# Hybrid decoder step: the recurrence's pairs 32 and 64 tokens apart in one round instead of two

## The chip, the cores and the metric

The kernel runs on one core of a Trainium2 chip. The metric is device time in microseconds (us) of one execution of the whole program. Of each kernel one execution was also recorded by the hardware profiler; its views are quoted below. PE is TensorE, DVE is VectorE, ACT is ScalarE, POOL is GpSimd, SP is SyncE, and PEld is TensorE's loading of weights.

## The reference

A two-layer decoder trunk over one prompt of 512 tokens and 8 samples of 4 tokens, 544 columns in all. Layer 0 mixes tokens by causal pooling, layer 1 by a gated linear recurrence (HGRN2) with 8 heads of 128 x 128 state; a gated ConvFFN follows each. The change lies in the recurrence of layer 1. Per head it computes, with `f` the gates, `k = 1 - f` up to bounds, and `b` the running sum of `log f`:

```python
b = jnp.cumsum(gc, axis=2)
o_inter = jnp.einsum('bhtd,bhde->bhte', qc * jnp.exp(b), S)
diff = b[:, :, :, None, :] - b[:, :, None, :, :]
decay = jnp.where(causal, jnp.exp(jnp.where(causal, diff, 0.0)), 0.0)
a = jnp.einsum('bhtd,bhsd,bhtsd->bhts', qc, kc, decay)
o = o_inter + jnp.einsum('bhts,bhse->bhte', a, vc)
```

So the score of a pair of tokens (t, s) is the product of q[t] and k[s] over 128 features, each multiplied by the product of all gates between s and t. The state S goes on from chunk to chunk with the chunk's whole gate product.

## The kernel before

Activations are kept transposed: features on the 128 partitions, tokens along the free axis. A projection block is a product of three TensorE matmuls per slice (helper `mm3`): weights and activations are split into a high and a low part in the float32r format, and high x high, high x low and low x high are added up. `block` runs that for 8 slices of 128 input features and two column halves of 256 and 288 columns, 48 matmuls into a tile `ps`. In the profile these are the rows with `ps<-xh,wh`, `ps<-xl,wh` and `ps<-xh,wl`.

The attention of a head works on four chunks of 128 tokens, tile `F` (gates), `K`, `q`, `v`. Decays are never divided out. Pairs are handled by their distance, in rounds that double: in the round of width w the chunk is cut into blocks of 2w tokens, and the K of the first half is multiplied with the q of the second half. `scale` then multiplies every second half of q with the gate product of the first half, and every first half of K with the product of the second, and `products` multiplies neighbouring gate products, so that `st["F"]` holds one product per block. `round_a` does distances up to 2 in one go (80 columns of a shared tile `q2`, called `z` there), `round_b` 4 and 8 (48 columns), and `level(w)` one width each: 16, 32, 64. A round's matmuls are plain float32 (two instructions each in the profile), and their 16, 32 or 64 output partitions make them use a column tile of TensorE: 32 or 64 of its 128 columns, at the position of their output partitions. In the profile's forms `128*32` is a matmul with 128 rows and a column tile of 32. ACT copies the scores to the tile `A` (128 x 4 x 128).

Behind the rounds, `ktrans` transposes K, `states` multiplies K with V (four full-width matmuls, `pa<-t` 128x128) and chains the chunks' states S on DVE, `output` adds A x V, q x S of the chunk before, and the samples' parts, which use `qm` and `As` on column tiles; then `sstates` and `back`.

The order of instructions isn't written out by hand. Every instruction is recorded in a list with its dependences and an estimated cost (`record`, `cost`), and `emit` goes through all engines with a simulated clock: of the instructions whose inputs and buffers are due first on an engine it takes the one with the longest remaining chain, and TensorE's recorded order counts as a part of that chain. The heads' stages are put into the list by `tick`, one of them for four `mm3` of the projection that runs meanwhile (`PACE` 0.25). So each engine's order is fixed when the program is built, and every engine works through its own list. All recorded instructions have the line of the one call in `emit`, L304.

Of the kernel before, what the change touches and what calls it, by code (L numbers as in the profile page):

```python
# [14 lines left out]
AF = _mybir.ActivationFunctionType  # L15
ALU = _mybir.AluOpType

P = 128
D = 1024
KT = 8  # L20
SEQ = 512
# [316 lines left out]
def trunk_step(ctx: ExitStack, tc: _tile.TileContext, xT, xp, xs, spool, s0, fctx, par, gb0, cst, bands,  # L338
# [3 lines left out]
    PE, DVE, ACT, POOL, SP = (plan.engine(*e) for e in (  # L342
        ("PE", nc.tensor), ("DVE", nc.vector), ("ACT", nc.scalar), ("POOL", nc.gpsimd), ("SP", nc.sync)))
# [10 lines left out]
    def tt(shape=(P, TOK), dt=F32):  # L354
        return tp.tile(list(shape), dt, tag="t", name="t")
# [7 lines left out]
    def ps1():  # L363
        return pap.tile([P, 512], F32, tag="pa", name="pa")
# [95 lines left out]
    def block(i, rH, rL, kc, cut=HT, tick=None):  # L460

        t = ps2()
        for k in range(kc):
            for hf, sl in enumerate((slice(0, cut), slice(cut, TOK))):
                mm3(t[:, hf, 0:sl.stop - sl.start], i, k, rH, rL, sl, k == 0, k == kc - 1)
                if tick:
                    tick()
        return t
# [544 lines left out]
    A = one.tile([P, 4, P], F32, name="A")  # L1013
# [33 lines left out]
    q2 = rp.tile([P, 17 * ROUND_A], F32, tag="fst", name="q2", bufs=1)  # L1047
# [26 lines left out]
    def chunk(t, c):  # L1074
        return t[:, c * P:(c + 1) * P]

    def samp(t):
        return t[:, SEQ:TOK]

    def attention(h):  # L1080

        d = hd[h]
        F, K, q, v = d["F"], d["K"], d["q"], d["v"]
        st = {}
# [6 lines left out]
        def stacked(out, t):  # L1091

            t3 = sm.tile([P, 3, NS], F32, tag="t3", name="t3", bufs=2)
            ACT.activation(t3, samp(t).unsqueeze(1).broadcast_to([P, 3, NS]), AF.Identity)
            PE.transpose(out[0:96, 0:P], t3.rearrange("p a c -> p (a c)"), ident)
# [15 lines left out]
        def oddv(t, w):  # L1111
            return t.rearrange("p (n r w) -> p n r w", r=2, w=w)
# [9 lines left out]
        def products(w):  # L1122

            f = st["F"].rearrange("p (n r) -> p n r", r=2)
            n = f.shape[1]
            fn = st["fl"][:, st["fo"]:st["fo"] + n]
            st["fo"] += n
            DVE.tensor_tensor(fn, f[:, :, 0], f[:, :, 1], op=ALU.mult)
            st["F"] = fn

        def scale(t, w, r, f):

            tv = oddv(t, w)[:, :, r, :]
            fv = f.rearrange("p (n r) -> p n r", r=2)[:, :, 1 - r:2 - r].broadcast_to(list(tv.shape))
            DVE.tensor_tensor(tv, tv, fv, op=ALU.mult)
# [97 lines left out]
        def level(w):  # L1233

            pl = ps1()
            for c in range(4):
                for j in range(0, P, 2 * w):
                    PE.matmul(pl[j:j + w, c * w:(c + 1) * w], chunk(K, c)[:, j:j + w], chunk(q, c)[:, j + w:j + 2 * w],
                              start=True, stop=True, skip_group_check=True)
            for j in range(0, P, 2 * w):  # L1240
                ACT.activation(A[j:j + w, :, j + w:j + 2 * w], pl[j:j + w, 0:4 * w].rearrange("p (c t) -> p c t", c=4), AF.Identity)
            scale(q[:, 0:SEQ], w, 1, st["F"])
            scale(K[:, 0:SEQ], w, 0, st["F"])
            products(w)

        def ktrans():
            pk, pk2 = ps1(), ps1()
            for c in range(4):
                PE.transpose(pk[:, c * P:(c + 1) * P], chunk(K, c), ident)
            stacked(pk2, K)  # L1250
            Kt = tt((P, 4, P))
            ACT.activation(Kt, pk.rearrange("p (c e) -> p c e", c=4), AF.Identity)
            Ks = tt((P, P), F32R)
            ACT.activation(Ks[0:96], pk2[0:96, 0:P], AF.Identity)
            DVE.tensor_tensor(Ks[64:96], pk2[64:96, 0:P], Ks[64:96].bitcast(F32), op=ALU.subtract)
            for a in range(2):
                ACT.activation(qm[:, a, :, a * NL:(a + 1) * NL],
                               samp(q)[:, a * HS:(a + 1) * HS].rearrange("p (g t) -> p g t", t=NL), AF.Identity)
            st["Kt"], st["Ks"] = Kt, Ks
# [57 lines left out]
        def back():  # L1317
# [7 lines left out]
                           pq2[:, 0:P].rearrange("p (g x) -> p g x", g=4)[:, :, 0:8].rearrange("p g (h t) -> p g h t", h=2), AF.Identity)  # L1325
            hd[h]["on"] = o

        return [load, transposes, round_a, round_b] + [lambda w=w: level(w) for w in (16, 32, 64)] + \
            [ktrans, states, output, sstates, back]

    def do_g(gx, h):
# [22 lines left out]
    def each_p(g, o, hf):  # L1354
        if hf == 0:
            ut[g] = tt()
        DVE.tensor_tensor(ut[g][:, HV[hf]], o, R1[:, HV[hf]], op=ALU.mult)
        if hf == 1:
            kind, h = hgrn_order[g]
            DO[kind](ut[g], h)  # L1360
            if kind == "i":
                pending.extend(attention(h))
            ensure(idx[g] + GRP_U)

    group(idx, rH, rL, KT, each_p, res0.hooks(), (4, 2), (4, 2), (0, 1, 2, 3))
    for kind, h in hgrn_order[GRP_U:]:
        i = hin_i[kind, h]
        ensure(i + LOOK)
        while kind == "g" and "on" not in hd[h]:
            pending.pop(0)()  # L1370
        pace[1] = PACE
        t = block(i, rH, rL, KT, HP, tick)
        DO[kind](proj(t), h)
        if kind == "i":
            pending += attention(h)
# [156 lines left out]
```

## Time and profile before

| | us |
|---|---|
| median of three executions | 1206.9 |
| their lowest and highest | 1206.26, 1206.91 |
| the profiled execution's own time | 1207.21 |
| its span, first to last instruction | 1205.4 |
| busy: PE, PEld | 1184.2, 1148.4 |
| busy: DVE, ACT, POOL | 784.5, 558.9, 214.1 |

The mean granted clock of TensorE is 0.994 of full speed. A row of the timeline gives start and duration in us, the engine, the line, what is written from what, the form and how many instructions were merged; a PE row's duration reaches beyond the next row's start, since matmuls are pipelined. Names have their buffer numbers left out, so `t` stands for many tiles of one pool (q, K, gates, states among them), `pa` for the small PSUM tiles and `ps` for the double ones. `q<-t` or `pa<-q,t` means the shared tile `q2`.

### The profile page before, as it was taken

What the parts mean: (1) busy time and instruction counts of PE and PEld (TensorE: products, weight loads), DVE (VectorE), ACT (ScalarE), POOL (GpSimd) and SP (SyncE); (2) the same over time, 40 slices, a digit from 0 to 9 for tenths busy, and PEclk for the clock granted to TensorE, in tenths of its full rate; (3) what the DMA queues carried; (4) which work ended last, traced back from release to release, by engine and by line L of the source; (5) the groups of instructions that cost most, each with busy time, mean ns of one, the idle gap of its engine ahead of it and who ended that gap; (6) DMA issues with size and microseconds to landing.
All of it is one profiled execution on the core that took longest, in us unless ns stands there. A gap on an engine that the chain in (4) does not pass through costs nothing.

```text
span 1205.4 us, 25491 instructions
## 1 busy us (share of the span) xinstructions
PE 1184.2 (98%) x10268; PEld 1148.4 (95%) x10268; DVE 784.5 (65%) x1809; ACT 558.9 (46%) x1131; POOL 214.1 (18%) x512
## 2 busy tenths in 40 slices
PE   8999999999999999999999999999999999999996
PEld 7899999999999997999999999999999999999995
DVE  6777733775377666688888895468752676357645
ACT  4655434443244454555555554546432444234441
POOL 3331101110011132111121120324100111011113
PEclk9999999999999999999999999999999999999998
DMA  9732222222222355432322223445222222322202
GB/s 321 167 90 71 89 88 88 88 78 90 97 88 97 96 145 132 107 100 100 106 96 74 74 94 109 129 71 140 89 88 88 88 82 77 105 88 84 77 30 75
DMA packets 43222, 120.39 MB, mean 100 GB/s; under 512 B 5338, under 2 KB 9818, under 8 KB 43096
## 3 DMA queue, kind: packets, MB, share of 16 engines
q1 hardware_dynamic: 30336, 91.71, 23.0%
q0 software_dynamic: 12624, 27.01, 9.4%
q8 instruction: 81, 1.33, 0.4%
q14 instruction: 37, 0.30, 0.1%
q10 hardware_dynamic: 144, 0.05, 0.0%
HBM read 110.79 MB, written 8.31 MB: 99 GB/s over the span
## 4 chain that ended last, share of the span: by engine, by line
PE 95%; DVE 2%; DMA 1%; ACT 0%; issue 0%; SPq 0%; DVEq 0%; POOL 0%; ACTq 0%; POOLq 0%
PE ps L304 75%; PE pa L304 18%; PE pr L304 2%; DVE t L304 1%; DVE m L304 1%; DMA t<-bands 1%; DMA k<-wup 0%; SPq L304 0%; DVE c L304 0%; ACT wh L304 0%; ACT m L304 0%; DVE x L304 0%; DVE Al L304 0%; DVEq L1513 0%; ACT t L304 0%
## 5 line engine op out<-in xcount | busy, mean ns | idle before, releaser
L304 ACT ACTIVATE wh<-raw 128x512 fp32r<-128x512 f32 (+1 forms) x312 | 193.0, 620 | 324.6 <-PE ps L304 313.7
L304 PE MATMUL ps<-xh,wh 128*128 128x256 f32 (+1 forms) x1072 | 312.3, 291 | 0.0
L304 PE MATMUL ps<-xl,wh 128*128 128x256 f32 (+1 forms) x1072 | 311.4, 291 | 0.0
L304 PE MATMUL ps<-xh,wl 128*128 128x256 f32 (+1 forms) x1072 | 307.2, 287 | 0.0
L304 DVE TENSOR_TENSOR wl<-raw,wh 128x512 fp32r<-128x512 f32 (+1 forms) x312 | 210.6, 676 | 136.2 <-ACT wh L304 132.1
L304 PE MATMUL ps<-t,wh 128*128 128x272 f32 x1184 | 223.4, 288 | 0.8 <-ACT m L304 0.7
L304 PEld LDWEIGHTS ps<-xl,wh 128*128 128x128 f32 x1072 | 201.8, 188 | 3.7 <-issue 1.4
L304 PEld LDWEIGHTS ps<-xh,wh 128*128 128x128 f32 x1072 | 202.1, 189 | 3.0 <-issue 1.7
L304 PEld LDWEIGHTS ps<-xh,wl 128*128 128x128 f32 x1072 | 202.2, 189 | 1.5 <-issue 1.3
L304 PE MATMUL ps<-oh,wl 128*128 128x256 f32 (+2 forms) x688 | 198.3, 288 | 0.0
L304 PE MATMUL ps<-k,wh 128*128 128x256 f32 (+2 forms) x688 | 198.1, 288 | 0.0
L304 PE MATMUL ps<-oh,wh 128*128 128x256 f32 (+2 forms) x688 | 198.0, 288 | 0.0
L304 PEld LDWEIGHTS ps<-t,wh 128*128 128x128 f32 x1184 | 185.6, 188 | 1.7 <-ACT m L304 1.1
L304 DVE TENSOR_TENSOR t<-t 128x512 f32<-128x512 f32 (+10 forms) x332 | 141.2, 453 | 55.5 <-ACT t L304 45.9
L304 PE MATMUL ps<-t,wl 128*128 128x272 f32 x592 | 170.5, 288 | 0.0
L304 DVE SCALAR_TENSOR_TENSOR t<-t,prm 128x560 f32<-128x560 f32 (+1 forms) x184 | 146.9, 802 | 35.4 <-ACT t L304 32.5
L304 POOL COPY fst<-t 128x16 f32<-128x16 f32 (+1 forms) x176 | 73.0, 450 | 440.6 <-DVE t L304 440.3
L304 DVE TENSOR_TENSOR t<-ps,R 128x512 f32<-128x512 f32 (+1 forms) x216 | 86.4, 434 | 76.6 <-PE ps L304 74.9
L304 PEld LDWEIGHTS ps<-k,wh 128*128 128x128 f32 x688 | 129.7, 189 | 0.5 <-issue 0.5
L304 PEld LDWEIGHTS ps<-oh,wh 128*128 128x128 f32 x688 | 129.8, 189 | 0.0
L304 PEld LDWEIGHTS ps<-oh,wl 128*128 128x128 f32 x688 | 129.3, 188 | 0.0
L304 ACT ACTIVATE t<-t 128x560 f32<-128x560 f32 (+4 forms) x137 | 83.0, 617 | 97.1 <-DVE t L304 96.1
(173 smaller groups left out, 1637.3 us busy)
## 6 DMA issues: line engine op xcount, KB each, us to landing
raw<-wup SPq DMA_DIRECT2D x78, 512.0 KB, 3.3
raw<-wdn SPq DMA_DIRECT2D x32, 448.0 KB, 3.3
raw<-win SPq DMA_DIRECT2D x26, 512.0 KB, 3.3
raw<-wdn SPq DMA_DIRECT2D x16, 512.0 KB, 3.2
wh<-wup POOLq DMA_DIRECT2D x16, 256.0 KB, 3.3
wl<-wup POOLq DMA_DIRECT2D x16, 256.0 KB, 5.2
t<-s POOLq DMA_DIRECT2D x16, 256.0 KB, 4.0
o_hs<-t POOLq DMA_DIRECT2D x16, 256.0 KB, 2.3
```

The lines of the kernel that those rows point to most:

```text
L304: o[1](*o[3], **o[4])
```

## The change

`level(32)` and `level(64)` are replaced by one stage, `round_c`. Instead of scaling q and K by the round of 32 before the pairs of 64 are formed, it prepares a tile z (in `q2`) per chunk with the q that each of the three quarter blocks of K needs, and computes both distances at once: K of tokens 0 to 31 meets 96 columns (tokens 32 to 63 unscaled, 64 to 127 multiplied by one more gate product), K of tokens 32 to 63 meets 64 columns, K of 64 to 95 meets 32 columns. These are three matmuls per chunk, on column tiles at 0, 32 and 64, 12 per head as before (8 and 4). One copy on ACT (`ends`) and one multiplication on DVE (the middle of z) are added per head; the copies to A stay three, the scalings of q and K four, the `products` two. A head has one stage fewer, 11 for 12.

```diff
+        def round_c():
+
+            w = 32
+            z = q2[:, 0:4 * P].rearrange("p (c t) -> p c t", c=4)
+            F32_ = st["F"].rearrange("p (c n) -> p c n", c=4)
+            qc = q[:, 0:SEQ].rearrange("p (c t) -> p c t", c=4)
+            ends = z.rearrange("p c (n t) -> p c n t", t=w)[:, :, 0::3]
+            ACT.activation(ends, qc.rearrange("p c (n r t) -> p c n r t", r=2, t=w)[:, :, :, 1, :], AF.Identity)
+            scale(q[:, 0:SEQ], w, 1, st["F"])
+            DVE.tensor_tensor(z[:, :, w:3 * w], qc[:, :, 2 * w:], F32_[:, :, 1:2].broadcast_to([P, 4, 2 * w]), op=ALU.mult)
+            pl = ps1()
+            for c in range(4):
+                o, k = 3 * w * c, chunk(K, c)
+                PE.matmul(pl[0:w, o:o + 3 * w], k[:, 0:w], z[:, c, 0:3 * w], start=True, stop=True, skip_group_check=True)
+                PE.matmul(pl[w:2 * w, o + w:o + 3 * w], k[:, w:2 * w], qc[:, c, 2 * w:], start=True, stop=True, skip_group_check=True)
+                PE.matmul(pl[2 * w:3 * w, o:o + w], k[:, 2 * w:3 * w], z[:, c, 3 * w:], start=True, stop=True, skip_group_check=True)
+            v = pl[:, 0:12 * w].rearrange("p (c t) -> p c t", c=4)
+            for j in (0, 2 * w):
+                ACT.activation(A[j:j + w, :, j + w:j + 2 * w], v[j:j + w, :, 0:w], AF.Identity)
+            ACT.activation(A[0:2 * w, :, 2 * w:], v[0:2 * w, :, w:], AF.Identity)
+            scale(K[:, 0:SEQ], w, 0, st["F"])
+            products(w)
+            scale(q[:, 0:SEQ], 2 * w, 1, st["F"])
+            scale(K[:, 0:SEQ], 2 * w, 0, st["F"])
+            products(2 * w)
...
-        return [load, transposes, round_a, round_b] + [lambda w=w: level(w) for w in (16, 32, 64)] + \
+        return [load, transposes, round_a, round_b, lambda: level(16), round_c] + \
```

The planner orders the whole stretch of the eight heads anew. Two places on PE follow; a row is the instruction, what it writes from what, the output's partitions and columns, and how many equal ones stand in a row. `pa<-q_862,t` is a matmul that reads z in `q2`.

The rounds of 32 and 64 in the sixth head, before, from the end of one run of projection matmuls to the next:

```order
L304 MATMUL pa<-t 32x32 x8
L304 MATMUL ps<-xl,wh 128x288
L304 MATMUL ps<-xh,wl 128x288
L304 MATMUL ps<-xh,wh 128x256
L304 MATMUL ps<-xl,wh 128x256
L304 MATMUL ps<-xh,wl 128x256
L304 MATMUL ps<-xh,wh 128x288
L304 MATMUL ps<-xl,wh 128x288
L304 MATMUL ps<-xh,wl 128x288
L304 MATMUL ps<-xh,wh 128x256
L304 MATMUL ps<-xl,wh 128x256
L304 MATMUL pa<-t 64x64 x4
```

The same place in the changed kernel:

```order
L304 MATMUL ps<-xh,wh 128x288
L304 MATMUL pa<-q_862,t 32x32 x4
L304 MATMUL ps<-xl,wh 128x288
L304 MATMUL pa<-t 32x64 x4
L304 MATMUL ps<-xh,wl 128x288
L304 MATMUL ps<-xh,wh 128x256
L304 MATMUL pa<-q_862,t 32x96 x4
L304 MATMUL ps<-xl,wh 128x256
```

The two runs of narrow matmuls have become three, each of the four chunks' matmuls of one column tile, with projection matmuls between them. In the eight heads 5, 6, 5, 2, 4, 1, 6 and 7 projection matmuls stand between the first and the second of the three, and 4, 2, 2, 2, 2, 2, 2 and 7 between the second and the third.

The output of the first head, before; the four `pa<-t` matmuls of `states` stand 12 projection matmuls ahead of the first `pa<-t,A` row:

```order
L304 MATMUL ps<-xh,wl 128x288
L304 MATMUL pa<-t,A 128x128 x4
L304 MATMUL pa<-t 128x128 x3
L304 MATMUL pa<-t,qm 32x128 x8
L304 MATMUL pa<-t,As 8x128 x4
L304 MATMUL ps<-xh,wh 128x256
```

The same place in the changed kernel, with the four matmuls of `states` in its first row:

```order
L304 MATMUL pa<-t 128x128 x4
L304 MATMUL ps<-xh,wl 128x288
L304 MATMUL pa<-t,A 128x128 x4
L304 MATMUL pa<-t 128x128
L304 MATMUL pa<-t,qm 32x128 x3
L304 MATMUL pa<-t 128x128
L304 MATMUL pa<-t,qm 32x128 x3
L304 MATMUL pa<-t 128x128
L304 MATMUL pa<-t,qm 32x128 x2
L304 MATMUL pa<-t,As 8x128 x4
```

The states' matmuls have moved next to the output, and the three products of q with S stand between the matmuls with `qm`. In the eight heads the rows with `qm` and `As` make 3, 2, 3, 3, 3, 2, 1 and 4 runs, one run each before; between the states' matmuls and the output stand 1, 2, 1, 8, 2, 0, 3 and 0 projection matmuls, 12 before.

## The prediction

> **What bounds the kernel now.** I read the page first, for the engine that carries the span, then the stretches in which the recurrence lies, then PE's waits there, and last PE's own timeline around the rounds that change.
>
> ```profile
> PE 1184.2 (98%) x10268; PEld 1148.4 (95%) x10268; DVE 784.5 (65%) x1809; ACT 558.9 (46%) x1131; POOL 214.1 (18%) x512
> PE 95%; DVE 2%; DMA 1%; ACT 0%; issue 0%; SPq 0%; DVEq 0%; POOL 0%; ACTq 0%; POOLq 0%
> ```
>
> PE is busy for 98% of the span and carries 95% of the chain of work that ended last. The recurrence of the eight heads runs from about 500 to 720 us. Three of its stretches (us, then busy time and count of PE, PEld, DVE, ACT, POOL, then granted clock, DMA share, GB/s):
>
> ```profile
> 560.00:580.00 20.00, 20.00 (x274) 18.39 (x273) 15.73 (x47) 12.09 (x38) 2.63 (x3) 1.00 0.28 96
> 660.00:680.00 20.00, 19.59 (x261) 17.99 (x253) 16.75 (x58) 10.50 (x36) 4.50 (x6) 1.00 0.16 55
> 700.00:720.00 20.00, 19.04 (x238) 17.55 (x237) 17.65 (x53) 11.09 (x35) 4.18 (x16) 1.00 0.24 75
> ```
>
> PE has no idle time in a usual stretch, at the full clock; the two worst ones lack 0.41 and 0.96 us. All waits of PE over 150 ns from 480 to 760 us are these two:
>
> ```profile
> PE pa L304 <- DVE q L304: 0.9, 1, 0.9
> PE pa L304 <- ACT t L304: 0.3, 1, 0.3
> ```
>
> So the projection's matmuls fill the time in which a head's rounds wait for ACT and DVE. What a shorter chain of rounds could give back is 0.9 + 0.3 = 1.2 us; whatever else moves the time is PE's own work and its order. That is what has to be priced.
>
> **The price of a piece on PE.** PE's timeline for the third head, start and duration in us. The round of 32 has 8 matmuls, the round of 64 has 4; each shows as two instructions, two passes over the same operands.
>
> ```profile
> 567.30 0.30 PE L304 MATMUL ps<-xh,wh 128*128 128x288 f32 x1
> 567.53 0.45 PE L304 MATMUL pa<-t 128*32 128x32 f32 x16
> 567.90 0.40 PE L304 MATMUL ps<-xl,wh 128*128 128x288 f32 x1
> 568.14 0.29 PE L304 MATMUL ps<-xh,wl 128*128 128x288 f32 x1
> ...
> 568.62 0.29 PE L304 MATMUL ps<-xh,wh 128*128 128x288 f32 x1
> 568.75 0.29 PE L304 MATMUL ps<-xl,wh 128*128 128x288 f32 x1
> 568.88 0.29 PE L304 MATMUL ps<-xh,wl 128*128 128x288 f32 x1
> ...
> 569.36 0.30 PE L304 MATMUL ps<-xh,wh 128*128 128x288 f32 x1
> 569.59 0.68 PE L304 MATMUL pa<-t 128*64 128x64 f32 x8
> 570.19 0.40 PE L304 MATMUL ps<-xl,wh 128*128 128x288 f32 x1
> 570.43 0.29 PE L304 MATMUL ps<-xh,wl 128*128 128x288 f32 x1
> ```
>
> Starts count here, not durations, which overlap. From the last full-width matmul before the round of 32 to the second one after it: 568.14 - 567.30 = 0.84 us. Undisturbed, the two steps take 568.88 - 568.62 = 0.26. The round costs 0.58. The round of 64: 570.43 - 569.36 - 0.26 = 0.81. What is removed is 1.39 us per head.
>
> Now the parts of such a price. Outside the piece: 0.23 from the last full-width start to the first narrow one (0.13 undisturbed) and 0.24 between the two full-width ones behind it (0.13), so 0.10 + 0.11 = 0.21 for going into a narrow column tile and out again. Inside: steps. Two passes on one tile follow each other; on different tiles they run side by side. The full-width rows give the step:
>
> ```profile
> 575.73 1.05 PE L304 MATMUL pa<-t,A 128*128 128x128 f32 x8
> 576.62 0.83 PE L304 MATMUL pa<-t 128*128 128x128 f32 x6
> 577.39 0.65 PE L304 MATMUL pa<-t,qm 128*32 128x128 f32 x16
> 577.96 0.40 PE L304 MATMUL pa<-t,As 32*8 32x128 f32 x8
> 578.29 0.38 PE L304 MATMUL ps<-xh,wh 128*128 128x256 f32 x1
> ```
>
> (576.62 - 575.73) / 8 = 0.111 us for 128 columns, 0.87 ns a column. So a step of 32 columns is 0.028, of 64 0.056, of 96 0.083. The round of 32 is then 8 steps on each of two tiles, 0.22 of its 0.37 (567.53 to 567.90); the round of 64, all on one tile, 8 steps, 0.44 of its 0.60. The rest, 0.15 and 0.16, is a piece's fixed inner cost. Two more pieces hold this up at widths on both sides of 64:
>
> ```profile
> 560.35 0.88 PE L304 MATMUL pa<-q,t 128*32 128x80 f32 x34
> 561.16 0.39 PE L304 MATMUL ps<-xh,wh 128*128 128x256 f32 x1
> ...
> 563.35 0.55 PE L304 MATMUL pa<-q,t 128*32 128x48 f32 x32
> 563.82 0.41 PE L304 MATMUL ps<-xl,wh 128*128 128x288 f32 x1
> ```
>
> Width 48: 32 instructions on four tiles, 8 steps of 0.042 = 0.33 of 0.47, rest 0.14. Width 80: 8 steps and two more of the odd 17th matmul, 10 x 0.069 = 0.69 of 0.81, rest 0.12. The 16 instructions with qm: 4 steps = 0.44 of 0.57 (577.39 to 577.96), rest 0.13. I take 0.14. **A piece costs 0.35 us plus its steps.**
>
> The Trainium skill, "TensorEngine Tiling (Array Packing)", section Tiling Modes, says that changing the tiling mode drains TensorE while changing the tile does not; it gives no figure, and the trace agrees, with 0.21 us around a piece. The same section says that different tiles load weights and multiply in parallel, which speaks for three tiles in one round; that holds only for tiles that stand beside each other in the order, and it is the third rival below.
>
> **The change, part by part.** (1) The new round in its place. As written, three matmuls per chunk lie on three column tiles and would run side by side. The order doesn't keep them so: the 32-wide ones need only ACT's copy, the 64-wide ones the scaled q, the 96-wide ones the multiplied middle of z as well, and each quartet is put where its own inputs are due. In all eight heads they stand as three pieces, with 1 to 7 full-width matmuls between. Each piece is four matmuls on one tile: 8 steps. 0.35 + 8 x 0.028 = 0.57; 0.35 + 8 x 0.056 = 0.80; 0.35 + 8 x 0.083 = 1.01. Together 2.38 against 1.39 removed: +0.99 per head, **+7.9 us** over eight.
>
> (2) The output. Before, qm and As stand as one piece per head (6 steps). Now the Kt matmuls stand closer to the output, and the three products of q with the states S, which wait for DVE's chain, are put between qm and As: 3, 2, 3, 3, 3, 2, 1 and 4 pieces in the eight heads, 21 for 8. Broken sets of four tiles also share less: counting, piece by piece, the passes on the fullest tile gives 64 steps for 48. A full-width matmul follows each piece here too, in the same number format; that going back costs the same shows at the start of the kernel:
>
> ```profile
> 22.11 1.03 PE L304 MATMUL pa<-pooled,t 128*128 128x256 f32 x4
> 23.06 0.64 PE L304 MATMUL pr<-t,cs 128*32 128x256 f32 x8
> 23.63 0.92 PE L304 MATMUL pa<-pooled,t 128*128 128x256 f32 x3
> ```
>
> Two steps of 256 (0.44) take 23.63 - 23.06 = 0.57, rest 0.13, as with qm. So 13 x 0.35 + 16 x 0.111 = 4.6 + 1.8 = **+6.4 us**. The lower bound for a piece that shares its drain with a neighbour is the inner 0.14 alone: 13 x 0.14 + 1.8 = 3.6.
>
> (3) One more ACT copy and one more DVE product per head, of 256 columns; the nearest rows:
>
> ```profile
> 564.21 0.40 DVE L304 TENSOR_TENSOR t<-t 128x256 f32<-128x256 f32 x1
> 566.62 0.43 ACT L304 ACTIVATE q<-t 128x272 f32<-128x272 f32 x1
> ```
>
> 0.40 x 8 = 3.2 us of DVE, 3.4 of ACT. Evacuations of A stay three per head, the scalings stay four. PE's work covers them: the stretches above leave DVE 2.3 to 4.3 us idle in 20, and PE's per-head time itself grows. Uncovered they would cost 3.2.
>
> (4) Waits. Up to 1.2 us can go. New ones can come: the 12 full-width matmuls that stood between the Kt matmuls and the output are now 0 to 8 of them.
>
> ```profile
> 573.35 1.05 PE L304 MATMUL pa<-t 128*128 128x128 f32 x8
> 574.56 0.26 ACT L304 ACTIVATE t<-pa 128x128 f32<-128x128 f32 x1
> 575.33 1.11 DVE L304 SCALAR_TENSOR_TENSOR t<-t,pa 128x128 f32<-128x128 f32 x3
> ```
>
> Here the states end 576.44 - 574.40 = 2.04 us after the Kt matmuls. Cover is left: the A matmuls (0.89), one or two q products (0.22 each), a piece or two. The shortest case, with nothing between, reaches the last q product after about 0.89 + 0.44 + 0.35 = 1.7, 0.4 late; without that cover up to 0.8 for each of seven heads, 5.6. Queued behind a waiting PE is the next projection block, whose evacuation feeds DVE, so nothing else gains. I take +0.5 net of what goes.
>
> Sum: 7.9 + 6.4 + 0.5 = 14.8. Against it: in two heads Kt and output stand as one run, and one return to the projection's matmuls (about 0.1) is saved in each: -0.2. The profiled execution took 1207.2 us (span 1205.4 and 1.8 around it); 1207.2 + 14.6 = 1221.8. It lies 0.3 above the median of 1206.9, so the forecast is **1221.5 us**. Its own range: pieces that share their drains take off 2.8 in the output and up to 1.7 in the round (8 x 0.21), the waits add up to 5.1: 1217 to 1227.
>
> **The rivals.** *The output's pieces are free* (chance 0.13): PE would have waited for the states there anyway, so filling in between costs nothing, and only the round counts: 1206.9 + 7.9 = 1214.8. For it: the order puts them there because S is late. Against: in the rows above S was in time.
>
> *The states are late* (0.12): PE waits the full 0.8 in seven heads, 5.6 in place of 0.5: 1226.6. For it: DVE has 17 to 18 us of work in 20 late in the stretch; against it, PE grows slower around it.
>
> *The tiles run side by side all the same* (0.03), the other side: if narrow matmuls behind a few full-width ones could start beside them, the round would cost 8 steps of 96 and one fixed price, 0.67 + 0.35 = 1.02 for 1.39: -0.37 x 8 = -3.0, and the output's pieces nothing: 1203.9. It decides where a quartet's start falls inside the quartet before it. Against: after each narrow piece the second full-width row comes 0.24 later, as no overlap would leave it.
>
> *The round is one piece in effect* (0.02): were side-by-side tiles to pay for half the output's pieces, -3.0 + 3.2, no change.
>
> **How the numbers follow.** Forecast 0.70, rivals 0.13, 0.12, 0.03, 0.02. Within 0.2% is 2.4 us, about what a measurement of this kernel can tell from no change. Slower: 0.70 + 0.13 + 0.12 = 0.95; no change 0.02; faster 0.03. The range, 1213 to 1228, takes in the first two rivals with the bounds of the round's price.
>
> **What would show it.** In the profile after: PE still near 98%, with some 13 us more span; per head three rows 128*32 with 32, 64 and 96 columns, x8 each, lasting to the next row about 0.37, 0.59 and 0.81; qm rows in several pieces, each with the 0.24 behind it. It is wrong if the three rows are one, if PE's waits on DVE in the output pass a microsecond per head, or if the span grows by less than 8 us.

## The result: 1.5% slower

The changed kernel takes 1225.03 us (median of four executions, 1224.71 to 1226.16), the kernel before, run beside it, 1206.7 (1206.26 to 1206.91): a ratio of 1.0154, with a 95% interval of 1.0142 to 1.0166. That is 18.3 us more, where 14.6 were forecast. The sign and the range held; the forecast of the size is short by a fifth. The profiled execution took 1225.24 us, its span 1223.4.

The page of the changed kernel, its busy times and the engines' shares of the chain of waits that ended last:

```profile
PE 1198.1 (98%) x10268; PEld 1154.9 (94%) x10268; DVE 791.9 (65%) x1817; ACT 562.0 (46%) x1139; POOL 214.0 (17%) x512
PE 91%; DVE 5%; ACT 1%; DMA 1%; issue 1%; SPq 0%; DVEq 0%; ACTq 0%
```

PE has as many matmuls as before and is busy 13.9 us longer (1198.1 for 1184.2): the pieces. The span grew by 18.0, so some 4 us are idle time of PE, and the chain says where to look: DVE's share rose from 2% to 5%.

The same stretches of the recurrence as before, and one more (busy time and count of PE, PEld, DVE, ACT, POOL, then granted clock, DMA share, GB/s):

```profile
560.00:580.00 20.00, 19.32 (x244) 17.10 (x242) 16.90 (x53) 10.89 (x32) 1.69 (x4) 1.00 0.30 94
640.00:660.00 20.00, 18.24 (x231) 16.42 (x230) 16.91 (x53) 10.41 (x28) 2.16 (x3) 1.00 0.26 89
660.00:680.00 20.00, 18.98 (x219) 17.49 (x218) 17.18 (x52) 10.30 (x34) 5.33 (x6) 1.00 0.25 84
700.00:720.00 20.00, 19.54 (x246) 18.13 (x245) 17.57 (x45) 12.29 (x32) 4.20 (x9) 1.00 0.36 122
```

The granted clock is 1.00 in each of these stretches, so it is no part of the difference. PE, which filled the stretch from 560 to 580 before, now lacks 0.68 us there, and 1.76 from 640 to 660. Its waits over 150 ns from 480 to 760 us (total, times, longest) were 1.2 us in two; now they are 4.7 us in twelve:

```profile
PE pa L304 <- DVE q L304: 2.0, 3, 1.0
PE pa L304 <- ACT q L304: 0.8, 2, 0.6
PE pa L304 <- ACT t L304: 0.7, 2, 0.4
PE pa L304 <- DVE t L304: 0.5, 2, 0.3
PE pa L304 <- DVE As L304: 0.4, 2, 0.2
PE pa L304 <- DVE Al L304: 0.3, 1, 0.3
```

Which matmuls wait is told by the groups of instructions with their shapes kept apart (busy time and mean, then idle time just before them and its releasers):

```profile
L304 PE MATMUL pa<-q,t 128*32 128x48 f32 x256 | 4.4, 208 | 2.7 <-DVE q L304 2.0 <-ACT t L304 0.7
L304 PE MATMUL pa<-q,t 128*32 128x32 f32 x64 | 3.5, 199 | 0.8 <-ACT q L304 0.8
L304 PE MATMUL pa<-t 128*16 128x16 f32 x256 | 3.1, 178 | 0.9 <-DVE As L304 0.4 <-DVE Al L304 0.3
```

The waits stand ahead of `round_b` (48 columns), of the round of 16 and of the first piece of `round_c`; the last 0.5 us (`DVE t`) stand ahead of the transposes of a head's output in `back`. None over 150 ns stands at the output's products with S.

**Where the 18 us lie.** I cut both traces at the first 80-column matmul of the first head and at the first matmul of the out-projection, and priced each narrow piece as the prediction does, less the time that PE waited there. Waits are those over 150 ns.

| us | before | after | difference | forecast |
|---|---|---|---|---|
| start of the kernel to the first round | 505.5 | 506.2 | +0.7 | 0 |
| recurrence, eight heads | 227.4 | 244.6 | +17.2 | +14.6 |
| - its rounds of 32 and 64, or `round_c` | 11.06 in 16 pieces | 18.48 in 24 | +7.4 | +7.9 |
| - `qm` and `As` in the output | 8.82 in 8 pieces | 14.78 in 21 | +6.0 | +6.4 |
| - PE waiting | 1.2 | 4.7 | +3.5 | +0.5 |
| - remainder | | | +0.3 | -0.2 |
| out-projection to the last matmuls of PE | 461.4 | 461.3 | -0.1 | 0 |

The 0.7 us at the start has nothing to do with the change: it is one wait there on DVE's `q`, 4.0 us before and 4.7 after, which was 2.3 in an experiment's run that leaves that part as it is.

The third head's round in the changed kernel, start and duration:

```profile
569.62 0.29 PE L304 MATMUL ps<-xl,wh 128*128 128x288 f32 x1
569.93 0.44 PE L304 MATMUL pa<-q,t 128*32 128x32 f32 x8
570.30 0.40 PE L304 MATMUL ps<-xh,wl 128*128 128x288 f32 x1
...
570.89 0.29 PE L304 MATMUL ps<-xh,wh 128*128 128x288 f32 x1
571.12 0.63 PE L304 MATMUL pa<-t 128*32 128x64 f32 x8
571.68 0.40 PE L304 MATMUL ps<-xl,wh 128*128 128x288 f32 x1
571.92 0.29 PE L304 MATMUL ps<-xh,wl 128*128 128x288 f32 x1
572.14 0.85 PE L304 MATMUL pa<-q,t 128*32 128x96 f32 x8
572.92 0.39 PE L304 MATMUL ps<-xh,wh 128*128 128x256 f32 x1
```

Three pieces, 0.37, 0.56 and 0.78 us from their first start to the next row (0.37, 0.59 and 0.81 were forecast), with the 0.24 behind each (571.68 to 571.92). The output of the first head:

```profile
521.04 1.05 PE L304 MATMUL pa<-t,A 128*128 128x128 f32 x8
521.93 0.39 PE L304 MATMUL pa<-t 128*128 128x128 f32 x2
522.24 0.42 PE L304 MATMUL pa<-t,qm 128*32 128x128 f32 x6
522.59 0.49 PE L304 MATMUL pa<-t 128*128 128x128 f32 x2
523.01 0.42 PE L304 MATMUL pa<-t,qm 128*32 128x128 f32 x6
523.36 0.49 PE L304 MATMUL pa<-t 128*128 128x128 f32 x2
523.78 0.41 PE L304 MATMUL pa<-t,qm 128*32 128x128 f32 x4
524.12 0.40 PE L304 MATMUL pa<-t,As 32*8 32x128 f32 x8
524.45 0.39 PE L304 MATMUL ps<-xh,wh 128*128 128x256 f32 x1
```

From the end of the A products to the projection it takes 524.45 - 521.93 = 2.52 us; the same instructions took 578.29 - 576.62 = 1.67 as one piece (the prediction's rows of the third head before the change). The q products (`pa<-t`, x2) do not wait.

### The profile page after: what moved, and what is told of

The parts are those of the page before. It is cut to its first block, busy times and chain, and to the rows that moved or that the text cites. A ratio compares the mean times of both kernels' runs of the same rounds, so it can differ in the third digit from the quotient of the medians.

```text
span 1223.4 us, 25532 instructions
## 1 busy us (share of the span) xinstructions
PE 1198.1 (98%) x10268; PEld 1154.9 (94%) x10268; DVE 791.9 (65%) x1817; ACT 562.0 (46%) x1139; POOL 214.0 (17%) x512
## 4 chain that ended last, share of the span: by engine, by line
PE 91%; DVE 5%; ACT 1%; DMA 1%; issue 1%; SPq 0%; DVEq 0%; ACTq 0%
PE ps L304 71%; PE pa L304 17%; DVE t L304 3%; PE pr L304 2%; DVE m L304 1%; DMA t<-bands 1%; DVE wl L304 0%; ACT t L304 0%; DMA k<-wup 0%; DVE o L304 0%; DVE Al L304 0%; ACT A L304 0%; DVE q L304 0%; ACT q L304 0%; ACT wh L304 0%
## 5 line engine op out<-in xcount | busy, mean ns | idle before, releaser
L304 PE MATMUL ps<-t,wh 128*128 128x272 f32 x1184 | 223.3, 288 | 0.8 <-ACT m L304 0.7
L304 DVE TENSOR_TENSOR t<-t 128x512 f32<-128x512 f32 (+7 forms) x332 | 143.8, 452 | 62.0 <-ACT t L304 46.1
```

The costliest lines, as they stand in the source:

```text
L304: o[1](*o[3], **o[4])
```

## The experiments

Each is timed beside the kernel before on the same chip, whose medians there were 1206.0 to 1206.4 us. A gain over the changed kernel is worked out from the two ratios to the kernel before, times 1206.7; their intervals leave it uncertain by some 2 us. Pieces are priced, the recurrence is cut and waits are counted as in the table above; the recurrence is of the one profiled execution, and leaves out what varies at the kernel's start. All of it stands together in a table behind the experiments.

### The two parts that PE pays for, undone one at a time

The planner takes an instruction when its inputs are due. A dependence on a later tile can so hold matmuls back and keep them together. First the round: all 12 of its matmuls also wait for the middle of z.

```diff
             for c in range(4):
                 o, k = 3 * w * c, chunk(K, c)
+                plan.after(z[:, :, w:3 * w])
                 PE.matmul(pl[0:w, o:o + 3 * w], k[:, 0:w], z[:, c, 0:3 * w], ...)
...  the same line ahead of the other two matmuls
```

> The changed kernel, with the twelve matmuls of the new round all held until the middle of z is written, so that they stand as one piece per head in the order they are written (96, 64, 32 columns, chunk by chunk); nothing is left out. Theory (a piece costs a fixed 0.35 us plus its steps, and tiles run side by side only inside a piece): the round falls from three pieces of 0.57 + 0.80 + 1.01 to one of 0.35 + 8 x 0.083 = 1.02 us per head, -10.9 us over eight; the output's pieces go from 21 to 23, +1.1. Forecast 1215 us, against 1225.0. Rival A (tiles of different widths don't overlap): the steps add up, 8 x 0.167 + 0.35 = 1.69 per head, -5.5 + 1.1, 1220.6. Rival B (the pieces were not the cost, the waits for DVE and ACT were): within 2 us of 1225.

Measured: 1216.65 us (1215.18 to 1219.02), ratio 1.0093 (1.0076 to 1.0110): 0.0061 x 1206.7 = 7.4 less than the changed kernel, where 10 were expected. PE's timeline of one head (single rows of the piece, its first and last):

```profile
512.46 0.27 PE L304 MATMUL pa<-q,t 128*32 128x96 f32 x1
512.47 0.24 PE L304 MATMUL pa<-t 128*32 128x64 f32 x1
512.47 0.25 PE L304 MATMUL pa<-q,t 128*32 128x32 f32 x2
...
512.98 0.33 PE L304 MATMUL pa<-q,t 128*32 128x96 f32 x2
513.24 0.39 PE L304 MATMUL ps<-xl,wh 128*128 128x256 f32 x1
```

All 24 instructions lie in 0.78 us, as long as the 96-column piece alone took above. The round costs 7.79 us over eight heads, 0.97 a head, where the three pieces cost 2.31 and the two rounds before 1.38. So the three column tiles do run side by side once they stand together, and the round by itself is then 3.3 us cheaper than what it replaces. The Trainium skill, "TensorEngine Tiling (Array Packing)", section Tiling Modes, has different tiles loading and multiplying in parallel; these rows agree. The pieces of the round give back 10.7 us, the recurrence only 7.3. Rival A, by which the round would cost 1.69 us a head, and rival B, by which nothing would be gained, both fall. The output breaks up further (23 pieces, +0.9), and PE now waits 2.5 us ahead of transposes, 1.7 of it ahead of those of K, which come right behind the round; in the changed kernel it waited 0.5 ahead of transposes and nothing ahead of K's.

Then the output: the `qm` and `As` matmuls also wait for the last state that is needed.

```diff
+                    plan.after(st["S"][:, 2, :])
                     # ahead of the matmul with qm, and the same ahead of the one with As
```

> The changed kernel, with the matmuls of qm and As held until the last state that the output needs is written, so that they stand as one piece per head; nothing is left out. The round stays in three pieces. Theory: 13 pieces and 16 steps fewer in the output, -6.3 us; the q products now stand alone between projection matmuls in thirteen places, about 0.1 for each return, +1.3. Forecast 1220 us against 1225.0. Rival (the output's pieces were free, since TensorE would have waited for the states): no change, 1225, with waits before the q products in the profile.

Measured: 1217.76 us (1217.11 to 1221.77), ratio 1.0106 (1.0089 to 1.0124), 5.8 less than the changed kernel. The output stands as 8 pieces again, 8.63 us, 6.1 less than in 21; `round_c` is untouched (18.49). The recurrence is 4.8 shorter, as PE waits 1.7 us ahead of transposes here, mostly those of a head's output. Putting work into the wait for S was no gain: the output's pieces are paid for, and holding them together makes PE wait for nothing there.

Both together:

> The changed kernel with both holds: the round one piece per head and the output's narrow matmuls one piece per head. Theory: the two add up, -10.9 - 6.3 and about +1.7 for q products that stand alone: 1209.5 us against 1225.0 of the changed kernel and 1206.7 of the kernel before; what is left above the kernel before is waits (6 us in the profile of the changed kernel for 3 before) less the 2.8 that one round of three tiles saves. Rival (waits grow as the pieces shrink, since the rounds' chain on DVE and ACT then is what lasts): above 1214.

Measured: 1210.46 us (1209.65 to 1212.42), ratio 1.0041 (1.0026 to 1.0056), 13.6 less than the changed kernel; the two gains add up (7.4 + 5.8 = 13.2). Pieces are 7.81 and 8.64, together 3.4 us less than before the change, and yet it is 4 to 5 us slower than before. Its waits of PE from 480 to 760 us:

```profile
PE pa L304 <- DVE t L304: 2.6, 6, 0.5
PE pa L304 <- DVE q L304: 2.0, 3, 1.2
PE pa L304 <- ACT wh L304: 1.3, 1, 1.3
PE pa L304 <- DVE As L304: 1.0, 4, 0.4
```

6.9 us, for 1.2 before. With PE's own cost gone, what is left of the loss is PE waiting for DVE and ACT, 3.9 of it (`DVE t`, `ACT wh`) ahead of transposes: 2.6 ahead of those of a head's output in `back`, 1.3 ahead of those of K.

### Does the written order decide whether tiles overlap?

In the kernel before, the round of 32 with its matmuls written tile by tile in place of chunk by chunk; nothing else moves.

```diff
-            for c in range(4):
-                for j in range(0, P, 2 * w):
+            for j, c in (...):        # j outside, c inside, where w is 32
```

> The kernel before, where the eight matmuls of the round of 32 are written tile by tile (four chunks on the first column tile, then four on the second) instead of alternating; they stay one piece, everything else keeps its place. It asks whether tiles must alternate in the order to run side by side. Theory (they must, or nearly): the piece takes 16 steps of 0.028 in place of 8, 0.60 us from its first start to the next row in place of 0.37, +1.8 us over eight heads, 1208.5. Rival (TensorE looks ahead past matmuls of one tile and overlaps them with those of another): the piece stays at 0.37 to 0.45, the time within 0.6 us of 1206.7.

Measured: 1207.17 us (1206.37 to 1211.7), ratio 1.0019 (1.0005 to 1.0033). The piece in the third head:

```profile
567.74 0.30 PE L304 MATMUL ps<-xh,wh 128*128 128x288 f32 x1
567.97 0.59 PE L304 MATMUL pa<-t 128*32 128x32 f32 x16
568.49 0.40 PE L304 MATMUL ps<-xl,wh 128*128 128x288 f32 x1
```

0.52 us, between the 0.37 of alternating tiles and the 0.60 of no overlap; over eight heads +1.15 us. The piece's length thus missed both expectations; the time, whose interval runs from 0.6 to 4.0 us above the kernel before, holds the +1.8 of the theory too and does not decide. In the trace's single records inside that row, which tell the tiles apart only by their spacing, the first tile's eight passes start some 32 ns apart from 567.97 to 568.21, and the second tile's first starts at 568.12, after the fifth of them: an overlap of three passes. So the next tile can start early, but not by far. With full-width matmuls between the quartets, as in the changed kernel, the pieces cost what no overlap would give: 2.31 us a head, for 2.38 in the forecast.

### The stage that is missing

A head with a stage fewer also moves everything behind the round to an earlier place in the list, since `tick` goes on at the same pace. The changed kernel with an empty stage in the freed place:

```diff
-        return [load, transposes, round_a, round_b, lambda: level(16), round_c] + \
+        return [load, transposes, round_a, round_b, lambda: level(16), round_c, lambda: None] + \
```

> The changed kernel with an empty stage behind the new round, so that a head has 12 stages again and the stages behind the round are put into the list where they stood before; no instruction is added. It asks whether the lost stage, not the new round itself, broke up the output. Theory: the output's narrow matmuls stand in 12 pieces (21 in the changed kernel), -4.3 us by 0.35 a piece and 0.111 a step; the round stays in three pieces; waits as in the changed kernel or fewer. Forecast 1220 us against 1225.0. Rival (the waits come from the round's longer chain and stay, while more room behind the round only moves them): 1222 or more.

Measured: 1216.18 us (1215.96 to 1218.82), ratio 1.0082 (1.0066 to 1.0098), 8.7 less than the changed kernel and 4 us under what was expected. The round is as costly as ever (18.49). The output falls from 21 pieces to 12 (14.78 to 10.69 us), and PE's waits from 4.7 to 2.8. So **most of the break-up of the output came from the lost stage, and not from the round itself**: the one line of the diff that shortens the list cost about as much as the round's three pieces (6.6 us of recurrence, for their 7.4). The expectation had counted on the pieces of the output and not on the waits.

With the round as one piece and two empty stages:

> The changed kernel with the round's twelve matmuls held into one piece and two empty stages behind the round, so that the stages behind it come later; no instruction is added. Theory: the round costs 1.02 us a head for 1.39 before (-2.9 over eight), the output stands in 10 pieces (+1.1 over the 8 of before), and with the K products due later than in the version with both holds its 5.6 us of waits ahead of the K transposes go; waits in all as in the kernel before or 2 us more. Forecast 1206 us, from 1204 to 1208, against 1206.7 of the kernel before and 1210.5 with both holds. Rival (the waits sit ahead of the rounds, where DVE is late, and the place of the stages behind them doesn't matter): 1209 to 1211.

Measured: 1208.73 us (1206.33 to 1210.67), ratio 1.0019 (1.0010 to 1.0029), about 2 us slower than the kernel before and above the expected 1204 to 1208. Pieces: 7.81 and, in ten, 9.65, together 2.4 less than before the change. The waits ahead of the transposes of K are gone, as the theory had it. But 3.6 us of waits remain, 2.4 more than before the change, and 2.3 of them stand in two places ahead of `round_b`, the largest 1.3 us: that part of the rival, DVE late ahead of the rounds, is borne out.

### What makes DVE late

The longest wait of the changed kernel's seventh head, from the timeline (in brackets the idle time ahead of a row, and its releaser):

```profile
675.20 2.59 POOL L304 TENSOR_TENSOR t<-t,cs 96x512 fp32r<-96x512 f32 x2 [2.74 <-DVE t L304]
676.81 2.03 DVE L304 TENSOR_TENSOR t<-t 128x4 f32<-128x4 f32 x4
678.77 0.41 DVE L304 TENSOR_TENSOR q<-t 128x256 f32<-128x256 f32 x1
679.32 0.55 PE L304 MATMUL pa<-q,t 128*32 128x48 f32 x32 [1.02 <-DVE q L304]
```

POOL multiplies here V of a head's samples with the block mask, in `sstates`. The row of 2.03 us merges four products of DVE of different shapes: in the single records the first, 128x4, takes 0.99 us, where it takes 0.16 without POOL, and the other three, of 256 and 272 columns, take their usual 0.41 to 0.43. The product that `round_b` waits for (`q<-t`) is queued behind them. The one long wait in the trace of before has the same company:

```profile
561.27 1.13 DVE L304 TENSOR_TENSOR t<-t 128x272 f32<-128x272 f32 x3 [0.79 <-PE pa L304]
...
697.73 2.81 POOL L304 TENSOR_TENSOR t<-t,cs 96x512 fp32r<-96x512 f32 x2 [3.20 <-DVE t L304]
698.65 2.53 DVE L304 TENSOR_TENSOR t<-t 128x272 f32<-128x272 f32 x3 [0.20 <-PE pa L304]
...
701.66 0.55 PE L304 MATMUL pa<-q,t 128*32 128x48 f32 x32 [0.87 <-DVE q L304]
```

Three DVE products (272, 256 and 272 columns) take 1.13 us alone and 2.53 beside POOL's. The single records show how: the two engines take turns. DVE's first product starts inside POOL's first and ends 0.30 us after it; the second starts inside POOL's second and ends 0.28 us after that; the third, beside none, takes 0.43. The other way round, each of POOL's two ends 0.90 us after the DVE product that was running when it started; left alone, one takes 1.03 to 1.06. So neither engine multiplies more slowly, but each product waits for the other engine's whole instruction. A DVE product that reads PSUM is not held: `t<-ps,R` of the changed kernel's eighth head takes 0.69 us inside a product of POOL, as elsewhere.

In the changed kernel three of the five waits ahead of `round_b` (sixth, seventh and eighth head) stand beside such a product of POOL; in the second and third head it is other work of DVE, a weight split of 0.69 us or five short products of 1.06 us together, that is queued ahead.

The test moves the product from POOL to ACT, which scales by the mask's column; first in the kernel before:

```diff
-                POOL.tensor_tensor(vb[0:96], st["Vst"][0:96].unsqueeze(1)..., cs[0:96, C_BM + 4 * s:...]..., op=ALU.mult)
+                for j in range(4):
+                    ACT.activation(vb[0:96, j, :], st["Vst"][0:96], AF.Identity, scale=cs[0:96, C_BM + 4 * s + j:C_BM + 4 * s + j + 1])
```

> The kernel before, with the samples' product of V and the block mask (two POOL instructions of 96 x 512 per head) done by ACT instead, eight instructions of 96 x 128 per head; the rounds keep their order. It asks what makes the three DVE products ahead of the 48-column round take 2.53 us in the eighth head (beside a POOL product) and 1.13 us in the third (beside none). Theory (POOL's product slows DVE's): the 2.53 falls to about 1.2, TensorE's wait of 0.9 us ahead of that round in the eighth head to under 0.2, and the time by 1 us or less, inside what three rounds can tell. Rival (the three products are slow for another reason, as an operand that comes late): they stay above 2 us and the wait stays.

Measured: 1203.15 us (1201.87 to 1205.07), ratio 0.9971 (0.9961 to 0.9981): faster than the kernel before by 3 us, where 1 or less was expected. The place of the wait:

```profile
696.15 1.14 DVE L304 TENSOR_TENSOR t<-t 128x272 f32<-128x272 f32 x3 [0.20 <-PE pa L304]
697.20 0.42 DVE L304 TENSOR_TENSOR q<-t 128x256 f32<-128x256 f32 x1
698.22 0.55 PE L304 MATMUL pa<-q,t 128*32 128x48 f32 x32
```

The three products are back at 1.14, and PE does not wait. No wait of PE over 150 ns is left from 480 to 760 us, and the recurrence falls from 227.4 to 224.4. The two waits were 1.2 of these 3.0 us; the rest lies in shorter ones, which that view leaves out, or in the order, and was not traced.

Then in the changed kernel, alone:

> The changed kernel with the samples' product of V and the block mask on ACT instead of POOL and nothing else changed; the round stays in three pieces, the output in 19. It asks how much of the changed kernel's waits (about 6 us of TensorE time in the recurrence, 3 in the kernel before) comes from POOL's products beside DVE's round products. Theory (POOL is most of it): waits fall to 2 us or less, two output pieces fewer give -1.2: 1225.0 - 4 - 1.2 = 1220 us. Rival (most of it is DVE's queue, with a weight split or an evacuation ahead of the round's products): waits stay at 4 us or more, 1222 or above.

Measured: 1216.6 us (1215.86 to 1216.95), ratio 1.0086 (1.0069 to 1.0102), 8.2 less than the changed kernel; both expectations were too high. The recurrence lost 6.9 us (237.7): 4.7 of waits, as none over 150 ns is left, and the output went from 21 pieces to 19 (13.94 us). The groups that waited:

```profile
L304 PE MATMUL pa<-q,t 128*32 128x48 f32 x256 | 4.4, 209 | 0.0
L304 PE MATMUL pa<-q,t 128*32 128x32 f32 x64 | 3.5, 199 | 0.1
L304 PE MATMUL pa<-t 128*16 128x16 f32 x256 | 3.1, 178 | 0.2
```

This pair is the cleanest look at the change. With no wait over 150 ns in either kernel it costs 237.7 - 224.4 = 13.3 us of recurrence: 18.47 - 11.06 = 7.4 for the round, 13.94 - 8.82 = 5.1 for the output, 0.8 beside. But it does not say how the waits came about: the move also changes the planner's order on DVE and ACT, and it took away the waits of the second and third head too, where POOL was not at work. How much of the 3.5 us of additional waits is DVE held up by POOL, and how much the order, stays open.

All of it together, the changed kernel with its round in one piece, two empty stages and the product on ACT:

> One piece per round, two empty stages behind it, and the samples' product of V and the block mask on ACT instead of POOL; nothing is left out. Theory: as the version with two empty stages, less the waits ahead of the 48-column round that stand beside POOL's products (1 to 2 us): 1205 us, at or below the 1206.7 of the kernel before. Rival (ACT's eight more instructions per head delay the rounds' copies by as much): equal to the version with two empty stages or slower.

Measured: 1202.19 us (1201.94 to 1203.26), ratio 0.9963 (0.9949 to 0.9978). It beats the kernel before by 0.4% and the changed one by 23 us. Beside the kernel before with the product on ACT alone (1203.15, intervals that overlap) the new round adds nothing that can be told apart: it saves 11.06 - 7.81 = 3.2 us, the output's two more pieces take 0.8 back, and the recurrences differ by 1.1 (224.4 and 223.3).

### All runs side by side

| us | recurrence | round | output (pieces) | waits | rest |
|---|---|---|---|---|---|
| before | 227.4 | 11.1 | 8.8 (8) | 1.2 | 206.3 |
| changed | 244.6 | 18.5 | 14.8 (21) | 4.7 | 206.6 |
| round held together | 237.3 | 7.8 | 15.7 (23) | 5.5 | 208.3 |
| output held together | 239.9 | 18.5 | 8.6 (8) | 5.4 | 207.4 |
| both held together | 231.4 | 7.8 | 8.6 (8) | 6.9 | 208.1 |
| one empty stage | 238.0 | 18.5 | 10.7 (12) | 2.8 | 206.0 |
| round together, two empty stages | 228.5 | 7.8 | 9.7 (10) | 3.6 | 207.4 |
| before, round of 32 tile by tile | 228.3 | 12.2 | 8.8 (8) | 1.2 | 206.1 |
| before, product on ACT | 224.4 | 11.1 | 8.8 (8) | 0 | 204.5 |
| changed, product on ACT | 237.7 | 18.5 | 13.9 (19) | 0 | 205.3 |
| round together, two empty stages, product on ACT | 223.3 | 7.8 | 9.7 (10) | 0.4 | 205.4 |

The rest is what the three columns leave of the recurrence. It moves by 4 us while the recurrence moves by 21, and it is smallest without the waits (204.5 and 205.3), which suggests that waits too short to be counted lie in it too; that was not traced. Three terms, the round's pieces, the output's and the waits, thus account for the runs to within those 4 us.

## Why the prediction was right, and where it was short

**Bound: right.** PE sets the time before and after; 13.9 of the 18 us are PE busier at the same count of matmuls and the same clock.

**Step 1, the round: right.** Three pieces in all eight heads, +7.4 us for +7.9. The fixed price of 0.35 and the steps of 0.028, 0.056 and 0.083 gave lengths within 0.03 us of the rows, though the single records put a 32-column step at 0.032 and not 0.028, and the fixed part lower by as much. That the loss is the breaking up and not the round was tested by holding it together: 0.97 us a head, for 2.31 in pieces. The 1.02 that the third rival gives for one round is so borne out, but only for tiles that stand together, as the prediction itself says; the rival's own mechanism, overlap across full-width matmuls, would have saved 3 us and was not seen.

**Step 2, the output: right.** 21 pieces, +6.0 us for +6.4. The rival that they are free fell: with one piece per head, the time fell by 5.8 us. What the prediction didn't name is why the order breaks there. It put the break-up down to the late states; one empty stage undid nine of the 13 additional pieces, so it was mostly the stage that the head lost.

**Step 3, one more copy and product: right.** ACT is busy 3.1 us longer, for 3.4 worked out. DVE is busy 7.4 longer, for 3.2. With POOL's product on ACT in both kernels the difference is 4.3 (783.2 for 778.9), so some 3 us of the excess go with POOL's product; the last one was not traced.

**Step 4, waits: this is the term that failed.** It was sized +0.5 us and measured +3.5, and it was put in the wrong place. The prediction looked for new waits at the q products with S, seven heads of up to 0.8; there PE has no wait over 150 ns. The waits stand in the next heads' rounds, at `round_b`, the round of 16 and the first piece of `round_c`, where a product of DVE or a copy of ACT is late. The prediction had the row that points there, the wait of 0.9 us on `q` before the change, and read it only as something that could go; it didn't ask what DVE was doing during that wait. And its cover, "DVE 2.3 to 4.3 us idle in 20", is a mean: it does not say that DVE is on time for one product with others queued ahead. That the range still held the result is in part luck: its upper part was there for waits at S, which did not come. The second rival, states late, came nearest in time (1226.6) by a mechanism that did not happen.

The waits are 3.0 us of the miss. The rest is the 0.7 us at the kernel's start, which varies from run to run, and 0.5 in the table's remainder, less the 0.9 by which steps 1 and 2 were over-priced.

## What to carry to other kernels

Column tiles of TensorE paid here only where their matmuls stood next to each other in the order that is emitted (0.97 us a head for 2.31); under a planner that starts what is due first, they need one common dependence, or each tile whose inputs are due at a time of their own becomes a piece at 0.35 us. When a stage is taken out of a paced list, count what moves behind it: here an empty stage in its place gave back 8.7 of 18.3 us. And follow even one wait of a microsecond to what the late engine was doing, since here that row led to the only gain that stands clear of the noise.

## What the hardware showed that was not expected

DVE and POOL, where both multiply two tensors in SBUF, take turns by whole instructions. DVE's three products took 2.53 us beside POOL's two and 1.13 without, and a product on 4 columns took 0.99 us for 0.16; POOL's pair took 2.81, where one alone takes 1.03 to 1.06. Moving POOL's part to ACT gave 3 us of 1206. The Trainium skill, "GPSIMD Engine Reference", Specifications, says that GpSimd's SBUF interfaces are shared with VectorE and contend with its instructions that have two SBUF inputs; the rows agree, and give it a size: what is left of the other engine's instruction.

The second tile's matmuls in the tile-by-tile order started before three passes of the first that are written ahead of them (568.12 against 568.21). The Trainium skill, "TensorE: Matmul & The Clock Gate", Part 3, says that matmuls start in program order without exception; on different column tiles the recorded starts here differ from that, by about 0.09 us, and it is by them that this document goes.
